# Banded attention: the meta keys' weights are transposed and multiplied last, the sample's loads get a step of their own, and the keys read their short block's product first

## The chip, the cores and the metric

The kernel runs on one core of one Trainium2 chip. The time is device microseconds (us) of one execution. Before the change the median of three runs is 2669.57 us (2669.01 to 2672.76). In the kernel's words PE is the engine of the matrix products, DVE the vector engine, ACT the scalar engine, POOL GpSimd, SP the queue that issues most transfers.

## What is computed

One step of a hybrid decoder trunk for 1024 prompt tokens behind 16 learned meta tokens, and for 8 sample sequences of 8 tokens, with the same weights: a half-step gated FFN, a token mixer (a gated delta rule branch A and a sliding-window attention branch B, merged by gates), and a second half-step FFN. The change touches the keys of branch A and all of branch B. Cut to these:

```python
# branch A, per head and chunk of c = 64 tokens
a_mat = where(strict, beta[..., :, None] * einsum('nzhid,nzhjd->nzhij', k, k) * decay, 0) + eye(c)
sol = triangular_solve(a_mat, rhs)          # the kernel inverts a_mat: its "lane solve"
# branch B, blocks of 128 queries: 16 meta keys, the block before, the own block, a sink
scores = concat([einsum('nbqkgd,nskd->nbkgqs', q, k_meta), einsum('nbqkgd,nbskd->nbkgqs', q, k_band)]) * scale
p = softmax(concat([where(mask, scores - slope * min(dist, 128), -inf), sink]))[..., :-1]
o = einsum('nbkgqs,nskd->nbqkgd', p[..., :16], v_meta) + einsum('nbkgqs,nbskd->nbqkgd', p[..., 16:], v_band)
y = sigmoid(gate_A) * o_A + sigmoid(gate_B) * o_B
```

There are 8 query heads of 128 on 2 key heads. The sample does the same with a cache of 128 past keys per sequence.

## The kernel before

A product in fp32 is made of three products of two-part operands (a high part and what is left of it, called the remainder here). Products that fill PE's time, the projections by weights (`gu`), are generators that yield after each matmul. `weave` takes several such generators, each with a stretch (a, b) and a count n, and interleaves their steps: `(g, 0.6, 1, 3)` puts three steps of g into the last 40% of the fill. So PE's program order is decided by these numbers and by the order of the yields. PE works in that order; the instructions of DVE, ACT and POOL are put in an order of their own by a scheduler that looks at the whole program, and each engine then works strictly in its order.

**Keys** (`keys`, `all_keys`, one head after another). For each head kT is transposed, its squared norms taken, and the Gram products of 9 token tiles weighted by the decay `dt`: `products(0)`, `products(4)` with four tiles each (PSUM tag `pk`), and `products(8)` for the short block of 80 tokens, whose Gram product already lies in a PSUM tile of tag `tr` (three buffers) with a transpose. DVE reads it there at L1058 (`b8`), and L1054 are the other eight tiles' reads. The next head's transposes (L1022) need a `tr` buffer.

**Banded attention** (`swa_block`, `swa_blocks`, `window`). There are 32 blocks: four passes p (two heads each) of 8 token blocks t. Block b does, in steps:

- scores: six matmuls (L1266 to L1268) into `sc`; DVE adds the distance term (L1269), takes the maximum (L1238) and its negative (L1239), ACT two exponentials (L1241), DVE a reciprocal (L1242), ACT two scalings (L1244); POOL splits the 16 meta weights into parts (`m3`, L1275 and L1276).
- meta: two transposes of `m3` (L1283) into a `pt` tile, which ACT copies out (L1285).
- own, then prev: two transposes (L1294) of the weights on the own and on the previous block into a `pt` tile each; ACT copies the high part out (L1296) and DVE the remainder (L1297, which reads `pt` and ACT's copy).
- po: the chain of seven matmuls (L1306) with the values into `po`; DVE multiplies by the gate (L1307).

Tag `pt` has two PSUM buffers, taken in turn: a third tile waits until all readers of the first are done. `swa_blocks` runs iteration i as: scores of block i, meta of block i-2, po of block i-3, own and prev of block i-2. In passes 0 to 2 these 5 steps are woven into 289 fill matmuls for 40 steps (7.2 each), in the last pass into 146 for 55 (the fill then takes 85% of the stretch).

Beside the blocks DVE does the lane solve (`lane_solve`, pairs of L1111 and L1113 of `ltmp` and `la`), until it is inverted and ACT copies it out in four parts (L1143). In passes 2 and 3 `swa_sample` is woven in, too: it loads queries (`q`, POOL's copies `qp`, L1332), scores of two halves (L1342), a softmax, then per half two transposes (L1357), the values' matmuls (L1366, L1369) into `po`, and a last transpose.

Of the kernel before, what the change touches and what calls it, by code (L numbers as in the profile page):

```python
# [13 lines left out]
ALU = mybir.AluOpType  # L14
# [4 lines left out]
P = 128  # L19
# [139 lines left out]
def steps_of(g, n):  # L159

    return itertools.islice(g, n)
# [573 lines left out]
class Mixer:  # L735
# [270 lines left out]
    def keys(self, h):  # L1006

        c, nc, pool = self.c, self.nc, self.kpool
        cv, dt = self.x[h]["cv"], self.x[h]["dt"]
        k8 = self.x[h]["k8"]  # L1010
        nc.sync.dma_start(self.kf_d[h][:, 0:1024], cv[:, 0:1024])
        nc.sync.dma_start(self.kf_d[h][:, 1024:NTOK], k8)
        kt = c.t(pool, [P, 9, P], tag="kt", bufs=2)
        sq = c.t(pool, [P, P], tag="sq", bufs=2)
        for t0 in (0, 4, 8):
            pt = self.ps([P, 4, P], "tr", 3)
            if t0 < 8:
                for t in range(t0, t0 + 4):
                    nc.tensor.transpose(pt[:, t - t0, :], cv[:, t * P:(t + 1) * P], self.k(C_IDENT))
                nc.scalar.copy(kt[:, t0:t0 + 4, :], pt)  # L1020
            else:
                nc.tensor.transpose(pt[:80, 0, :], k8, self.k(C_IDENT))  # L1022
                nc.tensor.matmul(pt[:80, 1, 0:80], k8, k8, start=True, stop=True)
                nc.gpsimd.memset(kt[64:P, 8, :], 0.0)
                nc.scalar.copy(kt[:80, 8, :], pt[:80, 0, :])
            if t0 < 8:
                yield
        ssq = c.t(pool, [P, 9], tag="ssq", bufs=2)
        for t in range(9):
# [12 lines left out]
        nc.gpsimd.tensor_tensor(out=nr, in0=nr, in1=c.half[:, 0:9], op=ALU.pow)  # L1042
        yield

        b = c.t(pool, [P, 8, P], tag="bm", bufs=2)

        def products(t0):
            if t0 < 8:
                pk = self.ps([P, 4, P], "pk", 2)
                for t in range(t0, t0 + 4):  # L1050
                    a = cv[:, t * P:(t + 1) * P]
                    nc.tensor.matmul(pk[:, t - t0, :], a, a, start=True, stop=True)
                for t in range(t0, t0 + 4):
                    nc.vector.scalar_tensor_tensor(out=b[:, t, :], in0=pk[:, t - t0, :], scalar=ns[:, t:t + 1],  # L1054
                                                   in1=dt[:, t, :], op0=ALU.mult, op1=ALU.mult)
            else:
                b8 = c.t(pool, [80, 80], tag="b8", bufs=2)
                nc.vector.scalar_tensor_tensor(out=b8, in0=pt[:80, 1, 0:80], scalar=ns[:80, 8:9], in1=dt[:80, 8, 0:80],  # L1058
                                               op0=ALU.mult, op1=ALU.mult)
                nc.sync.dma_start(self.b8_d[:, h, :], b8)  # L1060

        for t0 in (0, 4, 8):
            products(t0)
            if t0 == 8:
                for store in ((self.dt_d[h][:, 0:8, :], dt[:, 0:8, :]), (self.dt_d[h][0:80, 8, 0:80], dt[0:80, 8, 0:80])):
                    c.tc.keep_in_program_order(nc.sync.dma_start(*store))
                for half in range(2):
                    r = slice(half * 64, half * 64 + 64)
                    nc.sync.dma_start(self.la_d[h, :, half].rearrange("t r c -> r t c"), b[r, :, r])
                nc.sync.dma_start(self.bo_d[h], b[0:64, :, 64:128])  # L1070
            yield

    def all_keys(self):
        c = self.c
        with ExitStack() as ek:
# [3 lines left out]
            with ExitStack() as eg:  # L1079
# [6 lines left out]
                for h in range(H + 1):  # L1086
                    if 0 < h < H - 1:
                        self.sums(h + 1)
                    if 0 < h < H:
                        before.append((self.decays(h), 0.3, 0.4, 1))  # L1090
                    weave((fill[h], 0, 1, 73), *before)
                    if h < H:
                        self.keys_pack(h)
                    if h == 0:
                        self.sums(0)
                        self.sums(1)
                        drain(self.decays(0))
                    if h < H:
                        this = self.keys(h)
                        before = [(steps_of(this, 3), 0.03, 0.25, 3), (this, 0.6, 1, 3)]  # L1100


    def lane_solve(self, a, n, size, tmp):
# [142 lines left out]
    def swa_block(self, t, p, pool):  # L1246
# [31 lines left out]
        sg = c.t(pool, [P, 2, P], tag="sgb", bufs=2)  # L1278
        nc.sync.dma_start(sg, self.sg_d[hs, :, cols].rearrange("h p t -> p h t"))
        gs = slice(g * P, (g + 1) * P)  # L1280
        pt = self.ps([P, 4, P], "pt", 2)
        for i in range(2):
            nc.tensor.transpose(pt[:48, i, :], f32(m3[:, i]).rearrange("p a k -> p (a k)"), self.k(C_IDENT))  # L1283
        pm = self.pm[t % 2]
        nc.scalar.copy(pm[0:48], pt[:48, 0:2])  # L1285
        ops, late = [(self.vm[:, gs], pm)], []
        yield
        parts = [(own, t, "pto")]
        if t:
            parts.append((0, t - 1, "ptp"))  # L1290
# [10 lines left out]
            yield  # L1301
        if not t:
            yield
        po = self.ps([P, 4, P], "po")
        for k, (v, p_) in enumerate(ops + late):
            nc.tensor.matmul(po[:, 0:2], v, p_, start=k == 0, stop=k == len(ops + late) - 1)  # L1306
# [4 lines left out]
    def swa_blocks(self, pool):  # L1311
# [2 lines left out]
        part = lambda i, n: steps_of(bl[i], n) if 0 <= i < len(bl) else iter([None] * n)  # L1314
        for i in range(len(bl) + 3):
            yield from part(i, 1)
            yield from part(i - 2, 1)
            yield from part(i - 3, 1)
            yield from part(i - 2, 2)

    def swa_sample(self, g, pool, tmp):

# [12 lines left out]
        for half in range(2):  # L1335
            h4 = slice(4 * half, 4 * half + 4)
            kc = c.t(tmp, [P, 4, 152], tag="kc")
            nc.sync.dma_start(kc[:, :, 0:144], I["kcT"][:, g, h4])
            nc.gpsimd.tensor_copy(kc[:, :, 144:152], self.kn[:, g, 32 * half:32 * half + 32].rearrange("p (s t) -> p s t", t=8))
            ps = self.ps([P, 272], "sc", 2)  # L1340
            for i in range(4):
                nc.tensor.matmul(ps[32 * i:32 * i + 32, :152], qp[:, 4 * half + i, :], kc[:, i, :],  # L1342
# [37 lines left out]
    def window(self, pool, es):  # L1380
# [21 lines left out]
        for p in range(4):  # L1402
            side = []
            if p == 2:
                side = [(self.swa_sample(0, pool, c.pool(ss[0], "swat0")), 0, 1, 8)]
            if p == 3:
                el.close()
                self.hq = self.pcp = c.pool(es, "hq", side="right")
                self.pcs = 2
                fill = self.qv_steps(0, None)  # L1410
                side = [(self.swa_sample(1, pool, c.pool(ss[1], "swat1")), 0, 0.9, 8)]
            else:
                fill = solving(chained(*self.swa_q(2 * p + 2), *self.swa_q(2 * p + 3)), 0, 10)
            weave((fill, 0, 0.85 if p == 3 else 1, 146 if p == 3 else 289), (steps_of(blocks, 40 if p < 3 else 55), 0, 1, 40 if p < 3 else 55),
# [823 lines left out]
```

## Time and profile before

| | us |
|---|---|
| median of three runs | 2669.57 |
| the profiled execution's own time | 2665.62 |
| its span (first to last instruction) | 2663.8 |
| PE busy in it | 2593.7 |
| DVE busy | 1558.4 |
| ACT busy | 1130.7 |
| POOL busy | 1268.4 |

The rows that follow are of the profiled execution, with times in us from its start. The keys run about from 830 to 950, the blocks from 1010 to 1275. A row of a wait names the tile and line that waited, then the engine, tile and line that released it. A row of the timeline is: start, duration of one instruction, engine, line, operation, the tile written and the tile read, shape, and in brackets how long the engine was idle ahead of it and what ended that.

### The profile page before, as it was taken

How to read it: one execution, taken by the hardware profiler on the slowest of the kernel's cores; microseconds unless marked ns; L12 is line 12 of the kernel's file. 1: busy time of each engine (PE TensorE's matmuls, PEld its weight loads, DVE VectorE, ACT ScalarE, POOL GpSimd, SP SyncE). 2: the span in 40 equal slices, each digit the busy share in tenths (PEclk: the TensorE clock that was granted, in tenths of full speed). 3: DMA queues.
4: the chain of work that ended last, by engine and by line, in shares of the span. 5: the costliest groups of instructions: out<-in, count | busy, mean ns of one | idle time of the engine just before them, and what ended most of it. 6: DMA issues, size and time to landing. Idle time of an engine off the chain costs nothing.

```text
span 2663.8 us, 49377 instructions
## 1 busy us (share of the span) xinstructions
PE 2593.7 (97%) x18993; PEld 2475.1 (93%) x18993; DVE 1558.4 (59%) x2315; ACT 1130.7 (42%) x2728; POOL 1268.4 (48%) x1205
## 2 busy tenths in 40 slices
PE   7999999999999999999999999999899999999998
PEld 7999999999988999888889999997699999999998
DVE  7657565545677726995454444444466656554566
ACT  6333343432145634457444444454443434334221
POOL 6656555445524533433343333435565555554471
PEclk9999999999999999999999999999999999999999
DMA  4344343667544744335333333335443434338764
GB/s 164 121 152 152 127 167 117 242 227 253 190 151 151 230 148 130 106 122 176 98 106 88 89 95 99 100 93 160 138 132 140 167 127 149 127 137 319 244 225 145
DMA packets 231570, 406.48 MB, mean 153 GB/s; under 512 B 61814, under 2 KB 123414, under 8 KB 231046
## 3 DMA queue, kind: packets, MB, share of 16 engines
q1 hardware_dynamic: 211030, 324.75, 38.0%
q10 hardware_dynamic: 20304, 78.56, 7.5%
q8 instruction: 150, 2.46, 0.4%
q14 instruction: 86, 0.70, 0.1%
HBM read 264.36 MB, written 140.53 MB: 152 GB/s over the span
## 4 chain that ended last, share of the span: by engine, by line
PE 47%; DVE 1%; ACT 1%; POOL 1%; issue 1%; DMA 0%; POOLq 0%; DVEq 0%; SPq 0%; ACTq 0%
PE y L532 9%; PE B L352 7%; PE C L352 5%; PE A L352 4%; PE gu L132 4%; PE gu L128 4%; PE gu L130 4%; PE dn L128 1%; PE dn L132 1%; PE dn L130 1%; PE ch L1651 1%; PE tr L1527 1%; PE ch L1656 0%; PE oq L1646 0%; PE on L1673 0%
## 5 line engine op out<-in xcount | busy, mean ns | idle before, releaser
L132 PE MATMUL gu<-xh,wl 128*128 128x512 f32 (+3 forms) x1456 | 495.7, 340 | 0.0
L128 PE MATMUL gu<-xh,wh 128*128 128x512 f32 (+3 forms) x1456 | 491.9, 338 | 0.0
L130 PE MATMUL gu<-xl,wh 128*128 128x512 f32 (+3 forms) x1456 | 490.6, 337 | 0.0
L318 POOL TENSOR_TENSOR wl<-T,wh 128x512 fp32r<-128x512 f32 x246 | 330.5, 1350 | 314.1 <-ACT wh L317 244.4
L532 PE MATMUL y<-hb,wh 128*128 128x256 f32 (+2 forms) x2528 | 430.6, 290 | 2.1 <-ACT acc L572 1.0
L318 POOL TENSOR_TENSOR wl<-raw,wh 128x512 fp32r<-128x512 f32 x200 | 282.9, 1423 | 249.0 <-ACT wh L317 191.1
L532 PEld LDWEIGHTS y<-hb,wh 128*128 128x128 f32 x2528 | 366.1, 189 | 3.2 <-ACT acc L572 1.2
L317 ACT CAST wh<-T 128x512 fp32r<-128x512 f32 x246 | 152.2, 620 | 362.5 <-PE B L352 110.4
L132 PEld LDWEIGHTS gu<-xh,wl 128*128 128x128 f32 x1456 | 276.9, 190 | 16.4 <-issue 0.4
L130 PEld LDWEIGHTS gu<-xl,wh 128*128 128x128 f32 x1456 | 276.9, 190 | 16.3 <-issue 0.4
L128 PEld LDWEIGHTS gu<-xh,wh 128*128 128x128 f32 x1456 | 276.7, 190 | 16.4 <-issue 0.9
L532 PE MATMUL y<-hb,wl 128*128 128x256 f32 (+2 forms) x1264 | 271.8, 289 | 0.0
L317 ACT CAST wh<-raw 128x512 fp32r<-128x512 f32 x200 | 122.4, 621 | 276.8 <-PE C L352 81.9
L806 POOL TENSOR_TENSOR wl<-raw,wh 128x1024 fp32r<-128x1024 f32 x58 | 141.0, 2431 | 180.6 <-ACT wh L805 161.5
L543 DVE TENSOR_TENSOR acc<-acc,y 128x552 f32<-128x552 f32 (+4 forms) x216 | 144.9, 679 | 139.0 <-PE y L532 138.7
L532 PEld LDWEIGHTS y<-hb,wl 128*128 128x128 f32 x1264 | 207.1, 188 | 0.0
L292 DVE TENSOR_TENSOR T<-raw,raw 128x512 f32<-128x512 f32 x124 | 117.0, 948 | 107.1 <-POOL wl L318 107.1
L1606 POOL TENSOR_TENSOR f<-f,mhalf 128x1 f32<-128x1 f32 (+1 forms) x72 | 54.8, 762 | 125.5 <-DVE f L1604 119.2
L303 DVE TENSOR_TENSOR T<-raw,T 128x512 f32<-128x512 f32 x62 | 65.5, 1059 | 61.8 <-POOL wl L318 61.4
L292 DVE TENSOR_TENSOR T<-raw,T 128x512 f32<-128x512 f32 x62 | 63.3, 1028 | 31.9 <-POOL wl L318 31.5
L966 DVE SCALAR_TENSOR_TENSOR cv<-pc,cw,cv 128x1131 f32<-128x1131 f32 x48 | 66.8, 1393 | 21.4 <-POOL cv L963 20.8
L1111 DVE TENSOR_TENSOR ltmp<-la 72x14 f32<-72x14 f32 (+37 forms) x76 | 72.1, 948 | 12.3 <-DMA la<-b_d 11.4
(612 smaller groups left out, 7298.1 us busy)
## 6 DMA issues: line engine op xcount, KB each, us to landing
hb<-hid SPq DMA_DIRECT2D x71, 552.0 KB
hb<-hid SPq DMA_DIRECT2D x71, 544.0 KB
hid<-hs ACTq DMA_DIRECT2D x69, 552.0 KB
hid<-hs ACTq DMA_DIRECT2D x69, 544.0 KB
raw<-in_w_in_dram SPq DMA_DIRECT2D x58, 512.0 KB
raw<-in_ffn_w_gate_dram SPq DMA_DIRECT2D x100, 256.0 KB
raw<-in_ffn_w_up_dram SPq DMA_DIRECT2D x94, 256.0 KB
raw<-in_ffn_w_down_dram SPq DMA_DIRECT2D x88, 256.0 KB
```

The costliest lines, as they stand in the source:

```text
L128: nc.tensor.matmul(ps, wh, xh, start=first and i == 0, stop=False)
L130: nc.tensor.matmul(ps, wh, xl, start=False, stop=False)
L132: nc.tensor.matmul(ps, wl, xh, start=False, stop=last and i == n - 1)
L292: pin(self.nc.vector.tensor_tensor(out=b[name], in0=b[x], in1=b[y], op=ALU.subtract))
L317: self.nc.scalar.copy(hi, s)
L318: self.nc.gpsimd.tensor_tensor(out=lo, in0=s, in1=f32(hi), op=ALU.subtract)
L352: self.nc.tensor.matmul(self.view(ps, (i,)), w[a][:, k * P:(k + 1) * P], self.X[p][i][b][:, k, :], start=first and k + a + b == 0, stop=k ...
L532: self.nc.tensor.matmul(self.view(ps[d], (i,)), w[x][:, d * P:(d + 1) * P], hb[:, y, lo:hi], start=j + x + y == 0, stop=j == len(items) - ...
L543: dve = lambda out, x, y: nc.vector.tensor_tensor(out=out, in0=x, in1=y, op=ALU.add)
L806: low.tensor_tensor(out=lo, in0=raw, in1=f32(hi), op=ALU.subtract)
L966: nc.vector.scalar_tensor_tensor(out=cv, in0=pc[:, w:w + PADW], scalar=self.cw[:, j, w:w + 1], in1=cv, op0=ALU.mult, op1=ALU.add)
L1111: pin(nc.vector.tensor_tensor(out=t, in0=a[:n, 0:j, j:j + 1].to_broadcast([n, j, w]), in1=a[:n, j:j + 1, j + 1:size].to_broadcast([n, j, w ...
```

## The change

In `swa_block` the meta step is moved behind own and prev, and its product moves to the end of the chain of po. In `swa_blocks` an iteration becomes: scores i, po i-3, own i-2, prev i-2, meta i-2. In `swa_sample` a yield is added ahead of the first half's score matmuls, so the sample has one step more and all its later steps stand elsewhere in the fill. In `keys` the short block's read is emitted ahead of `products(0)`, the stores go with `products(4)`, and there are two steps for three, at 0.55 to 0.95.

```diff
         def products(t0):
-            if t0 < 8:
-                pk = self.ps([P, 4, P], "pk", 2)
...
-            else:
-                b8 = c.t(pool, [80, 80], tag="b8", bufs=2)
...
-        for t0 in (0, 4, 8):
-            products(t0)
...
+        b8 = c.t(pool, [80, 80], tag="b8", bufs=2)
+        nc.vector.scalar_tensor_tensor(out=b8, in0=pt[:80, 1, 0:80], scalar=ns[:80, 8:9], in1=dt[:80, 8, 0:80],
+                                       op0=ALU.mult, op1=ALU.mult)
+        nc.sync.dma_start(self.b8_d[:, h, :], b8)
+        products(0)
+        yield
+        products(4)
...
-                        before = [(steps_of(this, 3), 0.03, 0.25, 3), (this, 0.6, 1, 3)]
+                        before = [(steps_of(this, 3), 0.03, 0.25, 3), (this, 0.55, 0.95, 2)]
...
-        pt = self.ps([P, 4, P], "pt", 2)
-        for i in range(2):
-            nc.tensor.transpose(pt[:48, i, :], f32(m3[:, i]).rearrange("p a k -> p (a k)"), self.k(C_IDENT))
-        pm = self.pm[t % 2]
-        nc.scalar.copy(pm[0:48], pt[:48, 0:2])
-        ops, late = [(self.vm[:, gs], pm)], []
-        yield
+        ops, late = [], []
         parts = [(own, t, "pto")]
...
+        pt = self.ps([P, 4, P], "pt", 2)
+        for i in range(2):
+            nc.tensor.transpose(pt[:48, i, :], f32(m3[:, i]).rearrange("p a k -> p (a k)"), self.k(C_IDENT))
+        pm = self.pm[t % 2]
+        nc.scalar.copy(pm[0:48], pt[:48, 0:2])
+        late.append((self.vm[:, gs], pm))
+        yield
         po = self.ps([P, 4, P], "po")
...
             yield from part(i, 1)
-            yield from part(i - 2, 1)
             yield from part(i - 3, 1)
-            yield from part(i - 2, 2)
+            yield from part(i - 2, 3)
...
+            if not half:
+                yield
             ps = self.ps([P, 272], "sc", 2)
...
-                side = [(self.swa_sample(0, pool, c.pool(ss[0], "swat0")), 0, 1, 8)]
+                side = [(self.swa_sample(0, pool, c.pool(ss[0], "swat0")), 0, 1, 9)]
...
-                side = [(self.swa_sample(1, pool, c.pool(ss[1], "swat1")), 0, 0.9, 8)]
+                side = [(self.swa_sample(1, pool, c.pool(ss[1], "swat1")), 0, 0.9, 9)]
```

Line numbers shift with it: L1287 of the changed kernel is L1294 of before, L1299 is L1283, L1265 is L1266, L1142 is L1143, L1240 is L1241, L1243 is L1244, L1289 is L1296, L1301 is L1285, L1053 is L1054.

PE around block 12 (its weights are s_13027, its meta parts m_1949_13048), in the second pass, before; the lines left out are fill matmuls and the rest of each chain:

```order
L1283 MATMUL pt_13287<-ident_62,m_1949_13048 48x128 x2
...
L1306 MATMUL po_13300<-ptm_1643_11198,vm_11196 128x256
...
L1306 MATMUL po_13300<-ptpl_13225,vth_11193 128x256
...
L1294 MATMUL pt_13323<-ident_62,s_13027 128x128 x2
...
L1294 MATMUL pt_13337<-ident_62,s_13027 128x128 x2
...
L1266 MATMUL sc_13361<-kxh_11190,qbh_13355 128x272
...
L1283 MATMUL pt_13395<-ident_62,m_1969_13156 48x128 x2
```

The same place in the changed kernel:

```order
L1306 MATMUL po_13285<-ptpl_13212,vth_11193 128x256
L1306 MATMUL po_13285<-ptm_1643_11198,vm_11196 128x256
...
L1287 MATMUL pt_13306<-ident_62,s_13027 128x128 x2
...
L1287 MATMUL pt_13326<-ident_62,s_13027 128x128 x2
...
L1299 MATMUL pt_13340<-ident_62,m_1949_13048 48x128 x2
...
L1265 MATMUL sc_13361<-kxh_11190,qbh_13355 128x272
```

The meta transposes of a block moved from the step after the scores of two blocks on to the fourth step after them; own and prev stand one step earlier than they did, and the third `pt` tile in a row is now taken by meta two steps behind own.

ACT near the last copies of the lane solve (`ltmp`), where block 21's own and prev tiles are copied out (ptoh, ptph); s_2209 holds the weights of a later block; before:

```order
L1285 CAST ptm1_1643_11198<-pt_2216_14346 48x256
L1143 COPY ltmp_1633_11185<-la_1632_11184 128x1024
L1241 ACTIVATE s_2209_14312,dnb_2213_14325<-s_2209_14312,nmb_2212_14324 128x273 x2
L1244 ACTIVATE s_2209_14312<-s_2209_14312,dnb_2213_14325 128x272 x2
L1296 CAST ptoh_2222_14384<-pt_2221_14381 128x256
L1143 COPY ltmp_1633_11185<-la_1632_11184 128x1024
L1296 CAST ptph_2225_14398<-pt_2224_14395 128x256
```

and in the changed kernel:

```order
L1301 CAST ptm0_1642_11197<-pt_2205_14295 48x256
L1142 COPY ltmp_1633_11185<-la_1632_11184 128x1024
L1255 CAST qbh_2257_14521<-qb_2256_14519 128x256
L1227 ACTIVATE qe_2216_14354<-gu_2199_14267 128x256
L1240 ACTIVATE s_2209_14312,dnb_2213_14325<-s_2209_14312,nmb_2212_14324 128x273 x2
L1142 COPY ltmp_1633_11185<-la_1632_11184 128x1024
L1289 CAST ptoh_2220_14370<-pt_2219_14367 128x256
L1243 ACTIVATE s_2209_14312<-s_2209_14312,dnb_2213_14325 128x272 x2
L1289 CAST ptph_2224_14387<-pt_2223_14384 128x256
```

The last copy of the lane solve moved from behind own's copy `ptoh` to ahead of it.

DVE in the keys of head 0, where b_1472 and b_1469 are the short block's read, as a piece of the difference:

```order
 L1037 TENSOR_TENSOR sd_9799<-s__1445_9699,dec_9686 128x9
-L1054 SCALAR_TENSOR_TENSOR bm_9853<-pk_9854,ns__1446_9700,dt_9721 128x128 x2
+L1053 SCALAR_TENSOR_TENSOR bm_9849<-pk_9853,ns__1446_9700,dt_9721 128x128 x2
 L1038 TENSOR_TENSOR kt_9755<-kt_9755,sd_9799 128x1152
 L994 TENSOR_TENSOR dt_9723<-dt_9723,cst_9420 128x1024
 L996 TENSOR_TENSOR dt_9723<-dt_9723,cst_9420 80x80
-L1054 SCALAR_TENSOR_TENSOR bm_9853<-pk_9854,ns__1446_9700,dt_9721 128x128 x2
-L1054 SCALAR_TENSOR_TENSOR bm_9853<-pk_9872,ns__1446_9700,dt_9721 128x128 x4
-L1058 SCALAR_TENSOR_TENSOR b_1472_9891<-tr_9780,ns__1446_9700,dt_9721 80x80
+L1053 SCALAR_TENSOR_TENSOR bm_9849<-pk_9853,ns__1446_9700,dt_9721 128x128 x2
+L1053 SCALAR_TENSOR_TENSOR bm_9849<-pk_9879,ns__1446_9700,dt_9721 128x128 x3
+L1058 SCALAR_TENSOR_TENSOR b_1469_9850<-tr_9780,ns__1446_9700,dt_9721 80x80
```

Though it is written first, the short block's read stands only one tile's read earlier in DVE's order than before.

## Rows read from the trace of the kernel before

**Rows 1.** The page: busy us of each engine, share, instructions.

```profile
PE 2593.7 (97%) x18993; PEld 2475.1 (93%) x18993; DVE 1558.4 (59%) x2315; ACT 1130.7 (42%) x2728; POOL 1268.4 (48%) x1205
```

**Rows 2.** Waits of PE, 730 to 1285: us in total, times, longest.

```profile
PE pt L1283 <- POOL m L1276: 2.9, 2, 2.1
PE tr L1022 <- DVE b L1058: 2.7, 1, 2.7
PE sc L1342 <- POOL qp L1332: 2.7, 1, 2.7
PE po L1366 <- DVE sgb L1307: 2.0, 2, 1.4
...
PE pt L1357 <- ACT s L1244: 1.4, 1, 1.4
...
PE pt L1283 <- POOL m L1275: 0.7, 1, 0.7
PE pt L1283 <- DVE nms L1239: 0.7, 1, 0.7
PE pt L1283 <- DVE ptol L1297: 0.7, 1, 0.7
```

**Rows 3.** Windows: length, busy us of PE, PEld, DVE, ACT, POOL; clock; DMA.

```profile
1030.00:1092.00 62.00, 59.11 (x394) 55.09 (x393) 58.82 (x98) 29.17 (x90) 25.24 (x29) 0.97 0.37 115
1092.00:1154.00 62.00, 60.52 (x405) 55.25 (x405) 61.78 (x94) 32.09 (x98) 29.39 (x28) 1.00 0.37 116
```

**Rows 4.** Windows behind long waits of PE, same columns (clock is third from last).

```profile
847.48:850.88 3.40, 3.40 (x12) 2.83 (x11) 3.33 (x4) 1.74 (x8) 1.42 (x2) 0.50 0.95 241
1069.34:1072.74 3.40, 3.40 (x16) 3.40 (x15) 3.40 (x6) 0.36 (x1) 0.32 (x1) 0.50 0.40 118
1178.57:1181.97 3.40, 3.40 (x16) 3.32 (x15) 2.36 (x4) 1.37 (x4) 0.85 (x2) 0.50 0.45 127
1221.20:1229.00 7.80, 5.14 (x35) 4.17 (x36) 5.26 (x10) 2.86 (x11) 4.77 (x14) 1.00 0.83 242
```

**Rows 5.** Timeline of DVE in the keys of head 0.

```profile
844.69 1.63 DVE L1054 SCALAR_TENSOR_TENSOR bm<-pk,ns__1446_9700,dt 128x128 f32<-128x128 f32 x6
846.25 0.28 DVE L1058 SCALAR_TENSOR_TENSOR b<-tr,ns__1446_9700,dt 80x80 f32<-80x80 f32 x1
```

**Rows 6.** Timeline of PE and DVE: block 12's prev transposes, its own remainder.

```profile
1134.34 0.38 PE L1294 MATMUL pt<-ident,s 128*128 128x128 f32 x2
...
1137.44 0.42 DVE L1297 TENSOR_TENSOR ptol<-pt,ptoh 128x256 fp32r<-128x256 f32 x1
```

**Rows 7.** Timeline of PE, DVE and ACT at the first sample's softmax.

```profile
1172.54 0.29 PE L1268 MATMUL sc<-kxh,qbl 128*128 128x272 f32 x1
...
1174.04 0.92 DVE L1113 TENSOR_TENSOR la<-la,ltmp 128x686 f32<-128x686 f32 x1
...
1167.68 0.73 ACT L1244 ACTIVATE s<-s,dns 128x152 f32<-128x152 f32 x2 [2.52 <-DVE dns L1242]
```

**Rows 8.** Timeline of PE, ACT and POOL at the lane solve's last copy.

```profile
1216.22 0.38 PE L1294 MATMUL pt<-ident,s 128*128 128x128 f32 x2
...
1217.34 2.03 ACT L1143 COPY ltmp<-la 128x1024 f32<-128x1024 f32 x1 [0.36 <-DMA lrt_d<-ltmp]
1219.27 0.37 ACT L1296 CAST ptph<-pt 128x256 fp32r<-128x256 f32 x1
...
1223.05 0.76 POOL L1332 COPY qp<-q 128x64 f32<-128x64 f32 x4
```

**Rows 9.** Timeline of PE and ACT in the last pass: blocks 25 and 28.

```profile
1226.43 0.28 PE L1266 MATMUL sc<-kxh,qbh 128*128 128x272 f32 x1
1241.46 0.28 PE L1266 MATMUL sc<-kxh,qbh 128*128 128x272 f32 x1
...
1231.45 0.51 ACT L1241 ACTIVATE s<-s,nmb 128x273 f32<-128x273 f32 x1
1244.80 0.51 ACT L1241 ACTIVATE s<-s,nmb 128x273 f32<-128x273 f32 x1
```

More of the change, by code (lines that the diff above doesn't have):

```diff
@@ L1047, in products @@
         def products(t0):
-            if t0 < 8:
-                pk = self.ps([P, 4, P], "pk", 2)
[L1050 to L1055, printed above, removed]
-            else:
-                b8 = c.t(pool, [80, 80], tag="b8", bufs=2)
-                nc.vector.scalar_tensor_tensor(out=b8, in0=pt[:80, 1, 0:80], scalar=ns[:80, 8:9], in1=dt[:80, 8, 0:80],
-                                               op0=ALU.mult, op1=ALU.mult)
-                nc.sync.dma_start(self.b8_d[:, h, :], b8)
@@ L1062, in keys @@
-        for t0 in (0, 4, 8):
-            products(t0)
[L1064 to L1070, printed above, removed]
-            yield
+            pk = self.ps([P, 4, P], "pk", 2)
@@ new lines, in products @@
+            for t in range(t0, t0 + 4):
+                a = cv[:, t * P:(t + 1) * P]
+                nc.tensor.matmul(pk[:, t - t0, :], a, a, start=True, stop=True)
+            for t in range(t0, t0 + 4):
+                nc.vector.scalar_tensor_tensor(out=b[:, t, :], in0=pk[:, t - t0, :], scalar=ns[:, t:t + 1],
+                                               in1=dt[:, t, :], op0=ALU.mult, op1=ALU.mult)
+        b8 = c.t(pool, [80, 80], tag="b8", bufs=2)
+        nc.vector.scalar_tensor_tensor(out=b8, in0=pt[:80, 1, 0:80], scalar=ns[:80, 8:9], in1=dt[:80, 8, 0:80],
+                                       op0=ALU.mult, op1=ALU.mult)
@@ new lines, in keys @@
+        nc.sync.dma_start(self.b8_d[:, h, :], b8)
+        products(0)
+        yield
+        products(4)
+        for store in ((self.dt_d[h][:, 0:8, :], dt[:, 0:8, :]), (self.dt_d[h][0:80, 8, 0:80], dt[0:80, 8, 0:80])):
+            c.tc.keep_in_program_order(nc.sync.dma_start(*store))
+        for half in range(2):
+            r = slice(half * 64, half * 64 + 64)
+            nc.sync.dma_start(self.la_d[h, :, half].rearrange("t r c -> r t c"), b[r, :, r])
+        nc.sync.dma_start(self.bo_d[h], b[0:64, :, 64:128])
@@ L1280, in swa_block @@
         gs = slice(g * P, (g + 1) * P)
-        pt = self.ps([P, 4, P], "pt", 2)
-        for i in range(2):
-            nc.tensor.transpose(pt[:48, i, :], f32(m3[:, i]).rearrange("p a k -> p (a k)"), self.k(C_IDENT))
-        pm = self.pm[t % 2]
-        nc.scalar.copy(pm[0:48], pt[:48, 0:2])
-        ops, late = [(self.vm[:, gs], pm)], []
-        yield
+        ops, late = [], []
         parts = [(own, t, "pto")]
@@ L1339, in swa_sample @@
             nc.gpsimd.tensor_copy(kc[:, :, 144:152], self.kn[:, g, 32 * half:32 * half + 32].rearrange("p (s t) -> p s t", t=8))
+            if not half:
+                yield
             ps = self.ps([P, 272], "sc", 2)
```

## Prediction

> **What bounds the kernel now.** The page comes first: PE is busy 2593.7 of 2663.8 us, DVE 1558.4, ACT 1130.7 [rows 1]. Over the whole, PE is the bound, and a change that neither adds nor removes matmuls, as this one, can only move what PE waits. So the second view is PE's waits from the keys to the last block [rows 2]. Those the change can reach are: one of 2.7 us in the keys (next head's transposes behind the short block's read), meta transposes behind POOL (2.9 in two) and once each behind `m` of L1275, `nms` and `ptol` (0.7 each), the second sample's scores behind `qp` (2.7), the first sample's product behind `sgb` (2.0 in two), and its transposes behind the softmax (1.4). Together 13.8 us, half a per cent of the time, are at stake. The third view, the windows, shows that the stages differ: from 1092 to 1154 DVE is busy 61.78 of 62.00 us, and 58.82 in the 62 us ahead [rows 3]. There DVE's order decides, and PE's waits are symptoms. The fourth shows the clock: behind three of the waits the granted clock stands for 3.4 us at 0.50, the 1.2 GHz level, so each such stretch costs half of it, 1.7 us of work; behind the 2.7 us wait for `qp` it stays at 1.00, the 2.4 GHz level [rows 4].
>
> **The change part by part.** The sum is made against the profiled execution's own time of 2665.62 us, which lies 3.95 under the median of the runs, 2669.57.
>
> *Keys.* The same instructions remain. The short block's read stands in DVE's order behind the decay's last instruction as before, and one of the six tile reads ahead of it has gone behind. Six take 1.63 us [rows 5], so it comes 1.63 / 6 = 0.27 earlier: the wait of 2.7 shrinks to about 2.4, and I leave the slow clock behind it where it is. −0.3 us; the bounds are 0 and −4.4 (wait and slow stretch both gone: 2.7 + 1.7).
>
> *Meta last, in passes 0 to 2.* The two transposes, the ACT copy and the product of each block are only moved. What is new is which buffer they need. Of the two `pt` tiles in turn, meta of block b now takes the one of own of block b, two steps earlier, and so waits for DVE's remainder of own (L1297). Before, own's tile was taken again by the next block's meta, behind scores, po and the rest. Where DVE has slack this is nothing: a step is 7.2 fill matmuls, and 40 steps fill a pass. Where DVE is saturated it is late. Block 12 shows by how much: meta now stands where prev's transposes stood, at 1134.34, while own's remainder ended at 1137.44 + 0.42 = 1137.86 [rows 6]. That is 3.5 us later than PE would get there. Such a wait comes once and not per block, since in a stretch that DVE bounds, PE once late stays late by the same amount. Before, PE already stood 0.8 us for DVE's chain there (the second wait behind `m` of L1276, 2.9 − 2.1 [rows 2]), which the new wait contains: +3.5 − 0.8 = +2.7 us. The other meta waits (2.1 + 0.7 + 0.7) are part of PE's following DVE, and stay in another place. The bounds are −4.3 (2.1 + 0.8 + 0.7 + 0.7: DVE's order comes to suit the new place, all of them go) and +5.2 (3.5 in full, and one slow stretch of 1.7 behind it).
>
> *First sample.* With a ninth step its transposes stand right behind the scores that ran at 1172.54 [rows 7]. PE gets there at 1172.8 − 1.4 (the old wait is ahead no more) + 2.7 (the wait above) = 1174.1. In the changed DVE order the sample's reciprocal stands behind the solver's update of 686 elements, which ended at 1174.04 + 0.92 = 1174.96; the two scalings on ACT took 0.73, so the weights are ready at 1175.7 [rows 7]. New wait 1.6 for old 1.4: +0.2. The sample's product leaves the place right behind a block's po and comes 26 fills later (counted in PE's order before and behind, 691 to 717 from the first scores on), so that the waits for `sgb`, 2.0 [rows 2], go. I take −1.8; the bounds are −5.1 (1.4 + 2.0 + 1.7 for the slow stretch at 1178, which has then no wait ahead of it) and +2 (one more such stretch).
>
> *Block 21 and the lane solve's copies.* Meta of block 21 now stands where transposes ran at 1216.22. It needs own's copy on ACT, which now stands behind the solver's last copy: that began at 1217.34 and took 2.03, then a copy of 0.37 [rows 8] and a remainder of 0.42 [rows 6], ready at 1220.2. PE, late by the net of the terms above (−0.3 + 2.7 − 1.8 = +0.6), comes at 1216.8: +3.4 us. The scores of the second sample go from fill 870 to 886 of the same count, 16 fills on. The copies of `qp` end at 1223.05 + 0.76 = 1223.8 [rows 8], and 16 fills of a pass with 3 per step are five steps, a whole block, of which each takes 5.0 us there (below). So the wait of 2.7 goes. Net +0.7; bounds −2.7 (the copy hidden) and +3.4.
>
> *Last pass.* Scores of block 25 ran at 1226.43, of block 28 at 1241.46 [rows 9]: 15.03 / 3 = 5.0 us a block, so the four steps from the scores of block b+2 to the meta of b take 4.0. In ACT's changed order own's copy of b stands in five blocks (22, 23, 25, 26, 27) behind the exponentials of b+2. Those of block 28 ended at 1244.80 + 0.51 = 1245.31; with copy and remainder (0.37 + 0.42) meta could go at 1246.1, 4.6 after the scores: a wait of 0.6. Those of block 25 ended at 1231.96, which makes 6.3 and a wait of 2.3. I take the lower row, because a wait at one block lets ACT catch up for the next: 5 × 0.6 = 3.0, less the old wait for `nms` of 0.7 [rows 2]: +2.3. Bounds: −0.7 and 5 × 2.3 − 0.7 = +10.8.
>
> Sum: −0.3 + 2.7 − 1.8 + 0.7 + 2.3 = +3.6 us, 0.13%: 2665.6 becomes 2669.2, and the median 2673.2.
>
> Transfers are not changed: the short block's store and the others are issued in the same number, the first a little earlier, and no queue of theirs releases PE in [rows 2].
>
> **The rivals.** *The waits go and no new ones come (faster).* The schedule of DVE and ACT was made for the new order, and the rows above are read at the old one's times. If own's remainder is placed two solver instructions earlier (they take about 1 us each, as the 0.92 of [rows 7]), three quarters of block 12's lateness is gone, and there the sign turns. Then the meta waits (2.1 + 0.8 + 0.7 + 0.7 + 0.7 = 5.0), `qp` (2.7) and `sgb` (2.0) go: −9.7, 2659.9 on the median. For it speaks that each of them is a wait with one releaser which the change moves away from; against it the saturated window [rows 3].
>
> *The two buffers bind in every block of the last pass (slower).* If each of the five blocks waits as block 25's rows say, that term is +10.8 in place of +2.3, and the sum is +12.1: 2681.7. It decides from about 1 us a block on (5 × 1.0 − 0.7 and the other +1.3 are over 5.3). For it: PE's step is only 0.8 us there, less than a DVE or ACT hold-up of one long instruction (2.03 in [rows 8]). Against it: a late PE also gives ACT time. The Trainium skill, page "Perfetto Trace Analysis", section "Optimization Strategy", says that a gap that repeats on the engine that should be saturated can mean too little PSUM for the next tile, by its buffer count. By it this change, which brings the reuse of a two-buffer tile nearer to its readers, would show the same small gap in block after block; no row of before shows such a row of gaps, and whether the changed kernel does is what separates this rival.
>
> *It does nothing* (all new places hidden, old waits moved elsewhere): within 1 us of 2669.6. For it: most terms are differences of an old and a new wait of like size.
>
> **How the numbers follow.** My forecast +3.6 (its own range −1 to +6) gets 0.42, nothing 0.10, the faster rival 0.22, the slower one 0.26. A measurement of this kernel can tell about 0.2%, 5.3 us, from no change. The forecast and nothing lie within that (0.52 less a little for the forecast's upper edge, which about makes up for the rivals' weak forms), so: faster 0.22, same 0.50, slower 0.28. The range reaches to the middle of both rivals, 2660 to 2681, which leaves out half of each, 0.24; I keep it there, for weak forms of either fall inside.
>
> **What would show it.** Right: a wait of PE for `ptol` at the meta transposes (L1299 of the changed kernel) of 2 to 4 us near 1120 to 1140, and one near 1220 behind ACT's copy out of the lane solve; several of 0.3 to 1 us at the meta transposes after 1230; no wait for `qp` or `sgb`; a wait of about 2.4 still at the keys' transposes behind `b`. Wrong: no wait at the meta transposes at all (faster rival), over 1.5 us at most of them after 1225 (slower), more or fewer than three or four stretches at clock 0.50, each worth 1.7 us, or a keys' wait that is gone because DVE reaches the short block ahead of `dt`'s last part.

## The result, and the profile after

The changed kernel takes 2678.41 us (median of 7 runs, 2673.3 to 2680.93) against 2669.57 for the kernel before in the same session: a ratio of 1.0033, 95% interval 1.0024 to 1.0042. It is 8.8 us slower. That is inside the stated range (2660 to 2681), but beyond the 0.2% up to which the prediction spoke of "same", its largest chance, and above the forecast's own range (+3.6, with −1 to +6).

The page of the changed kernel, busy us of each engine, answers to [rows 1]:

```profile
span 2674.0 us, 49361 instructions
PE 2596.8 (97%) x18993; PEld 2474.6 (93%) x18993; DVE 1559.8 (58%) x2315; ACT 1132.6 (42%) x2728; POOL 1269.3 (47%) x1205
```

The work is the same, the span is 10.2 us longer (2674.0 for 2663.8). To see where, I take the start of the same fill matmul (the n-th projection matmul, 4752 in each) in both traces, at the borders of the stages:

```text
place                                   before     after   after - before
end of FFN1                             760.93    761.14   +0.21
keys done, ahead of the blocks         1010.06   1009.64   -0.42
ahead of the sample's second scores    1162.32   1163.91   +1.59
first sample's product done            1189.99   1191.16   +1.17
blocks 18 to 20 done                   1214.39   1218.46   +4.07
second sample's first scores           1227.18   1231.69   +4.51
last block done                        1291.89   1299.42   +7.53
end of the next stage                  1662.97   1670.17   +7.21
```

So 8.0 us arise between the blocks' start and their end (from −0.42 to +7.53). The other 2.7 of this pair of executions come after 1820 us, in code that the change doesn't touch. The profiled execution of before lies 3.95 under its median, so that the medians' 8.8 is the better number for the whole and the table for the places.

PE's waits in the blocks' stretch (1005 to 1285; us in total, times, longest), which answer to [rows 2]:

```profile
PE pt L1299 <- DVE ptol L1290: 8.4, 9, 2.0
PE pt L1299 <- ACT pts L1362: 3.0, 2, 1.7
PE sc L1343 <- POOL m L1274: 2.1, 1, 2.1
PE pt L1299 <- DVE nmb L1238: 2.1, 2, 1.3
PE pt L1299 <- DVE ptpl L1290: 1.1, 1, 1.1
PE pt L1299 <- DVE dnb L1241: 1.0, 1, 1.0
PE pt L1287 <- DVE sg L1377: 0.4, 1, 0.4
```

The waits for `qp`, `sgb` and the sample's softmax are gone, as are those for `m`. In their place the meta transposes (L1299) wait 15 times, 15.6 us in all: 8.4 + 3.0 + 2.1 + 1.1 + 1.0. In nine of them the releaser named is the remainder of own (`ptol`), the last reader of the tile that was filled two steps earlier. It is the true one in three more: the rows name `dnb` or `nmb`, which a meta transpose doesn't read, but own's remainder ends 0.14 to 0.15 ahead of these transposes, too (at 1083.34, 1091.37 and 1265.31, for starts at 1083.49, 1091.51 and 1265.46). The other three, 4.1 us, are for prev's tile (below). So all fifteen are waits for a tile to come free, twelve for own's (11.5 us), three for prev's.

The stretches at half clock from the keys to the last block, which answer to [rows 4] (the clock is the third number from the right):

```profile
846.97:850.38 3.41, 3.41 (x12) 2.82 (x11) 3.34 (x4) 1.77 (x8) 1.43 (x2) 0.50 0.91 241
1167.82:1171.23 3.41, 3.41 (x13) 2.98 (x12) 2.96 (x8) 1.12 (x4) 0.54 (x1) 0.50 0.67 216
1222.43:1225.85 3.42, 3.38 (x13) 3.17 (x14) 0.73 (x2) 2.47 (x7) 1.69 (x4) 0.50 1.02 293
```

Three, as before. The one at 1069 has gone with its wait, the one at 1178 stands at 1168, and one has come behind block 21's wait.

The keys, DVE and PE, which answer to [rows 5]:

```profile
844.45 1.37 DVE L1053 SCALAR_TENSOR_TENSOR bm<-pk,ns__1446_9700,dt 128x128 f32<-128x128 f32 x5
845.75 0.28 DVE L1058 SCALAR_TENSOR_TENSOR b<-tr,ns__1446_9700,dt 80x80 f32<-80x80 f32 x1
...
846.18 0.28 PE L1022 MATMUL tr<-ident,k 128*80 128x128 f32 x1 [2.43 <-POOL kt L1024]
```

Five tile reads stand ahead of the short block's in place of six, and the wait is 2.43 for 2.73: the 0.3 forecast. The bracket names a memset on POOL, but PE starts 0.15 after the short block's read ends (845.75 + 0.28 = 846.03), as it did before (846.25 + 0.28, then 846.68): the releaser is still `b`.

The saturated stretch: meta of block 10 and what it waits for, which answer to [rows 6]:

```profile
1119.07 0.38 PE L1299 MATMUL pt<-ident,m 128*48 128x128 f32 x2 [1.50 <-DVE ptol L1290]
...
1117.42 1.17 DVE L1110 TENSOR_TENSOR ltmp<-la 128x990 f32<-128x990 f32 x1
1118.50 0.42 DVE L1290 TENSOR_TENSOR ptol<-pt,ptoh 128x256 fp32r<-128x256 f32 x1
```

Here the forecast's mechanism is seen in one place: the remainder stands behind a solver product, ends at 1118.92, and PE goes on 0.15 later. Before, it stood behind the same product, which came 1.5 us later:

```profile
1118.91 1.19 DVE L1111 TENSOR_TENSOR ltmp<-la 128x990 f32<-128x990 f32 x1
1120.02 0.42 DVE L1297 TENSOR_TENSOR ptol<-pt,ptoh 128x256 fp32r<-128x256 f32 x1
```

And block 12, whose rows the forecast was made from:

```profile
1136.73 0.38 PE L1299 MATMUL pt<-ident,m 128*48 128x128 f32 x2 [1.17 <-DVE ptol L1290]
...
1136.18 0.40 DVE L1290 TENSOR_TENSOR ptol<-pt,ptoh 128x256 fp32r<-128x256 f32 x1
```

The first sample, whose second half's scores now follow block 18's scores by four fill matmuls ([rows 7] is of its softmax):

```profile
1167.12 0.47 PE L1343 MATMUL sc<-kc,qp 128*32 128x152 f32 x8 [2.12 <-POOL m L1274]
...
1163.50 3.17 DVE L1110 TENSOR_TENSOR ltmp<-la 128x752 f32<-128x752 f32 x1
1166.59 0.77 DVE L1268 SCALAR_TENSOR_TENSOR s<-scst,sc 128x272 f32<-128x272 f32 x2
...
1163.49 2.38 POOL L806 TENSOR_TENSOR wl<-raw,wh 128x1024 fp32r<-128x1024 f32 x1 [4.61 <-ACT wh L805]
```

The bracket again names the wrong one (`m` isn't read by this matmul). What it needs is a score tile: both were taken by block 18, and DVE reads the first of them only at 1166.59, behind a solver product of 3.17 us. The products of 782 and 720 elements around it took 0.96 and 0.90; this one began 0.01 after a weight split on POOL. Behind the wait comes a stretch at half clock. Such a meeting isn't new; the trace of before has one near there, at which PE did not need a score tile (DVE, then POOL):

```profile
1163.37 2.58 DVE L1111 TENSOR_TENSOR ltmp<-la 128x782 f32<-128x782 f32 x1
...
1162.72 2.41 POOL L806 TENSOR_TENSOR wl<-raw,wh 128x1024 fp32r<-128x1024 f32 x1 [7.34 <-ACT wh L805]
```

Block 19, with a tile of the sample between its prev and its meta (PE, then ACT, then DVE):

```profile
1199.56 0.38 PE L1287 MATMUL pt<-ident,s 128*128 128x128 f32 x2
1200.21 0.27 PE L1358 MATMUL pt<-ident,s 128*128 128x128 f32 x1
...
1202.90 0.38 PE L1299 MATMUL pt<-ident,m 128*48 128x128 f32 x2 [1.72 <-ACT pts L1362]
...
1199.24 2.02 ACT L1142 COPY ltmp<-la 128x1024 f32<-128x1024 f32 x1
1201.17 0.93 ACT L1243 ACTIVATE s<-s,dnb 128x272 f32<-128x272 f32 x2
1202.00 0.35 ACT L1289 CAST ptph<-pt 128x256 fp32r<-128x256 f32 x1
...
1202.38 0.42 DVE L1290 TENSOR_TENSOR ptpl<-pt,ptph 128x256 fp32r<-128x256 f32 x1 [2.59 <-ACT ptph L1289]
```

The sample's transposes (L1358) took own's tile in the turn of two, so meta has to take prev's, which was written 0.7 us ahead of the sample's and not two steps earlier. Prev's copy waits on ACT behind a copy of the lane solve of 2.02 and two scalings, the remainder ends at 1202.80, and PE goes on at 1202.90.

Block 21, which answers to [rows 8]:

```profile
1222.47 0.59 PE L1299 MATMUL pt<-ident,m 128*48 128x128 f32 x2 [2.01 <-DVE ptol L1290]
...
1219.65 1.94 ACT L1142 COPY ltmp<-la 128x1024 f32<-128x1024 f32 x1 [1.71 <-DMA lrt_d<-ltmp]
1221.50 0.36 ACT L1289 CAST ptoh<-pt 128x256 fp32r<-128x256 f32 x1
...
1221.89 0.42 DVE L1290 TENSOR_TENSOR ptol<-pt,ptoh 128x256 fp32r<-128x256 f32 x1 [3.10 <-ACT ptoh L1289]
```

This is the chain of the forecast, step for step: solver's last copy, own's copy, remainder, meta.

The last pass, which answers to [rows 9]:

```profile
1246.64 0.38 PE L1299 MATMUL pt<-ident,m 128*48 128x128 f32 x2 [1.27 <-ACT pts L1362]
1265.46 0.38 PE L1299 MATMUL pt<-ident,m 128*48 128x128 f32 x2 [1.31 <-DVE nmb L1238]
...
1263.66 1.32 DVE L970 SCALAR_TENSOR_TENSOR qv<-th,qv 128x1131 f32<-128x1131 f32 x1
1264.90 0.41 DVE L1290 TENSOR_TENSOR ptol<-pt,ptoh 128x256 fp32r<-128x256 f32 x1
```

Two waits of 1.3 and two of 0.2 and 0.4, not one in every block. The first stands again behind a tile of the sample, the second behind own's remainder (the bracket names `nmb`), which itself stands behind a long DVE instruction of the next stage.

### The profile page after: what moved, and what is told of

The parts are those of the page before. It is cut to its first block, busy times and chain, and to the rows that moved or that the text cites. A ratio compares the mean times of both kernels' runs of the same rounds, so it can differ in the third digit from the quotient of the medians.

```text
span 2674.0 us, 49361 instructions
## 1 busy us (share of the span) xinstructions
PE 2596.8 (97%) x18993; PEld 2474.6 (93%) x18993; DVE 1559.8 (58%) x2315; ACT 1132.6 (42%) x2728; POOL 1269.3 (47%) x1205
## 4 chain that ended last, share of the span: by engine, by line
PE 47%; POOL 1%; issue 1%; DMA 1%; ACT 1%; DVE 1%; SPq 0%; DVEq 0%; POOLq 0%; ACTq 0%
PE y L532 8%; PE B L352 7%; PE C L352 5%; PE A L352 4%; PE gu L132 4%; PE gu L128 4%; PE gu L130 4%; PE dn L128 1%; PE dn L132 1%; PE dn L130 1%; PE tr L1528 1%; PE ch L1652 1%; PE on L1674 1%; PE oq L1647 0%; PE ch L1657 0%
## 5 line engine op out<-in xcount | busy, mean ns | idle before, releaser
L805 ACT CAST wh<-raw 128x1024 fp32r<-128x1024 f32 x60 | 62.9, 1049 | 36.4 <-PE gu L130 36.4
```

## The experiments

Theory A, which I held on seeing this: meta's new place asks for a PSUM tile soon after its last readers, and that lateness is the cost; the sample's tiles in the same turn shorten it further. Theory B: the sample's new step is what costs. All runs are against the kernel before in the same session; a ratio of 0.001 is 2.7 us. The microseconds given behind a ratio are worked out from it and differ from the difference of the medians by up to 2.

**The parts alone.** First the attention blocks' order alone, on the kernel before:

```diff
-        ops, late = [(self.vm[:, gs], pm)], []
-        yield
+        ops, late = [], []
...
+        late.append((self.vm[:, gs], pm))
+        yield
         po = self.ps([P, 4, P], "po")
...
-            yield from part(i - 2, 1)
             yield from part(i - 3, 1)
-            yield from part(i - 2, 2)
+            yield from part(i - 2, 3)
```

> The kernel before with the new order in the attention blocks alone (meta turned and multiplied last; sample and keys as before). Theory A, the tile: meta's transposes now wait for DVE's remainder of own in one of the two pt buffers, and that is most of the change's cost; it expects +5 to +8 us on before, with eight or more waits of PE for ptol at the meta transposes, in the trace some 8 us in total. Theory B, the sample: its new step costs most (a wait of 2.1 for the score tile and 3.0 for its copies pts), so this kernel is at most +3 us.

Measured 2675.23, ratio 1.0021 (1.0012 to 1.0029), +5.6 us. PE's waits there, 820 to 1330:

```profile
PE pt L1300 <- DVE ptol L1291: 8.7, 9, 1.9
...
PE sc L1342 <- POOL qp L1332: 2.2, 1, 2.2
PE pt L1357 <- ACT s L1244: 1.9, 1, 1.9
PE pt L1357 <- DVE ptol L1291: 1.7, 1, 1.7
```

The nine waits for `ptol` are there without the sample's edit, and the sample's two old waits remain. Theory A holds for this part, at the lower end of what it expected.

The sample's step alone:

```diff
+            if not half:
+                yield
...
-                side = [(self.swa_sample(0, pool, c.pool(ss[0], "swat0")), 0, 1, 8)]
+                side = [(self.swa_sample(0, pool, c.pool(ss[0], "swat0")), 0, 1, 9)]
```

> The kernel before with the sample's extra step alone. Theory A: -3 to +1 us on before: the wait for qp (2.7) goes, and what comes at other places of the sample is no more than that. Theory B: +4 to +7 us, with waits of PE at the sample's scores and at transposes behind its copies, and a stretch at half clock behind the longest.

Measured 2667.39, ratio 0.9987 (0.9979 to 0.9996), 3.5 us faster. Theory B falls as it was stated: by itself the step helps. What it costs beside the new order is a question of its own (below).

The keys alone:

```diff
-        for t0 in (0, 4, 8):
-            products(t0)
...
+        nc.sync.dma_start(self.b8_d[:, h, :], b8)
+        products(0)
+        yield
+        products(4)
...
-                        before = [(steps_of(this, 3), 0.03, 0.25, 3), (this, 0.6, 1, 3)]
+                        before = [(steps_of(this, 3), 0.03, 0.25, 3), (this, 0.55, 0.95, 2)]
```

> The kernel before with the edit of the keys alone. Both theories: within 1 us of before, the wait at the second head's transposes about 2.4 in place of 2.7. A third, that the keys cost (another slow stretch, a later store): +2 us or more.

Measured 2670.76, ratio 1.0003 (0.9994 to 1.0011): nothing. And the whole change with the attention order of before put back:

```diff
-        ops, late = [], []
+        ops, late = [(self.vm[:, gs], pm)], []
+        yield
...
             yield from part(i, 1)
+            yield from part(i - 2, 1)
             yield from part(i - 3, 1)
-            yield from part(i - 2, 3)
+            yield from part(i - 2, 2)
```

> The changed kernel with the attention blocks' order of before: the edits of keys and sample alone. By the single runs -3 us against before (-3.4 for the sample, 0 for the keys), if nothing between these two adds to it.

Measured 2668.16, ratio 0.9995 (0.9986 to 1.0003), −1.3 us with an interval that takes in both −3 and nothing. What matters is the sum: alone, the parts make +5.6 − 3.5 + 0.8 = +2.9 us; together +8.8. About 6 us come from the edits meeting; by the intervals of the four runs that could be 1 to 11, so it needed a run of its own (the sample's tiles, below). Said by this run: the order costs 5.6 alone, and 1.0033 − 0.9995 = 0.0038, 10.1 us, where the sample's step and the keys are there, too.

**The tile.** To take meta off the pair, its transposes were written into the free half of prev's tile:

```diff
-        pt = self.ps([P, 4, P], "pt", 2)
         for i in range(2):
-            nc.tensor.transpose(pt[:48, i, :], f32(m3[:, i]).rearrange("p a k -> p (a k)"), self.k(C_IDENT))
+            nc.tensor.transpose(pt[:48, 2 + i, :], f32(m3[:, i]).rearrange("p a k -> p (a k)"), self.k(C_IDENT))
```

> The changed kernel, but meta's transposes are written into the free half of prev's pt tile, so that meta takes no buffer of its own and doesn't wait for own's remainder; all else as changed. Theory A: the waits of meta for ptol, ptpl and pts (12.5 us in the trace) go or shrink to what the softmax leaves, and the time falls by 5 to 9 us below the changed kernel, to that of before or a little under. If it is DVE's and ACT's lateness itself that PE follows, whatever the tile, or the sample's step (theory B), it falls by less than 3 us.

Measured 2703.73, ratio 1.0133 (1.0119 to 1.0147), +35.5 us. My expectation was wrong. PE's waits, 820 to 1330:

```profile
PE pt L1298 <- DVE ptpl L1290: 32.5, 24, 3.4
PE pt L1298 <- DVE ptol L1290: 4.4, 3, 1.6
```

Columns that nobody reads don't help: meta's write still waits for the readers of the other half of that tile, and these are now one step behind and not two. As an experiment on distance it is clear: two steps cost 8.4 us in nine waits, one step 32.5 in 24.

Then meta in the one buffer of `po`, whose last reader (the gate's product) belongs to a step three earlier, so that own and prev have the pair for themselves:

```diff
-        pt = self.ps([P, 4, P], "pt", 2)
+        pt = self.ps([P, 4, P], "po")
         for i in range(2):
             nc.tensor.transpose(pt[:48, i, :], f32(m3[:, i]).rearrange("p a k -> p (a k)"), self.k(C_IDENT))
```

> The changed kernel, but meta's transposes take the one buffer of po (read by the gate's product three steps earlier) and not a pt tile; own and prev then have the two pt tiles for themselves, and a tile is taken again a whole block later. Theory A, the tile: meta's waits for ptol, ptpl and pts (12.5 us in the changed kernel's trace) mostly go, some come back at po behind ACT's copy of meta or at meta behind the gate's product; 4 to 9 us below the changed kernel. If PE only follows DVE's and ACT's lateness, whatever the tile: within 2 us of the changed kernel, with waits of the same size at po for own's remainder.

Measured 2673.96, ratio 1.0014 (1.0006 to 1.0023): +3.7 us on before, some 5 below the changed kernel. PE's waits, 1005 to 1285:

```profile
PE po L1306 <- ACT ptm L1301: 6.0, 7, 2.1
PE po L1367 <- ACT ptm L1301: 2.5, 1, 2.5
```

No meta transpose waits for a remainder, but the chain of po now waits for ACT to have emptied meta's tile: less, not nothing.

**The sample's tiles.** The sample's transposes in score tiles, all else as changed:

```diff
-            pt = self.ps([P, 4, P], "pt", 2)
+            pt = self.ps([P, 272], "sc", 2)[:, 0:256].rearrange("p (a b) -> p a b", b=P)
...
-            px = self.ps([P, 4, P], "pt", 2)[:, 0]
+            px = self.ps([P, 272], "sc", 2)[:, 0:P]
```

> The changed kernel, but the sample's transposes take score tiles (tag sc) and not pt tiles. The two edits made alone sum to about +2 us and together to +8.8. If that is since the sample's tile comes between prev and meta in the turn of two, so that meta takes prev's tile one step behind it (waits behind ptpl and pts, 4.1 us in the trace): 3 to 6 us below the changed kernel. If the sum comes from the order that DVE and ACT got, and not from the tile: within 2 us of the changed kernel.

Measured 2674.6, ratio 1.0013 (1.0005 to 1.0022): +3.5 on before, 5.3 below the changed kernel, near the 6 us that the edits' meeting had cost. Not all of that gain need be the meeting's: in the old order the same move stands at 0.9981 (below) against 0.9987 for the sample's step alone, 1.6 us, though these two are not told apart. PE's waits from 1185 to 1238, the changed kernel first, then this one:

```profile
PE pt L1299 <- DVE ptol L1290: 2.0, 1, 2.0
PE pt L1299 <- ACT pts L1362: 1.7, 1, 1.7
PE pt L1299 <- DVE ptpl L1290: 1.1, 1, 1.1
```

```profile
PE pt L1299 <- DVE ptol L1290: 1.6, 2, 0.8
```

The waits behind prev are gone with the sample's tile from the turn, block 21's is 0.8 for 2.0, and the half-clock stretch at 1222 is not there (in this execution another stands at 1294, behind the blocks). The sample's own wait of 2.1 at its second scores is the same as before the move. Both moves at once:

> Both of the last two: meta in po's bank, the sample in score tiles, so that own and prev alone use pt. By theory A it is the fastest of the kernels with the new order, 6 to 11 us below the changed kernel, and at or under before. If po's single buffer, which now carries three kinds of tiles, binds: no better than with meta alone moved.

Measured 2672.41, ratio 1.0011 (1.0003 to 1.002): 5.9 below the changed kernel, not told apart from either alone, and not under before. The po chain's waits for `ptm` are the same (5.7 in seven, and 2.4 at the sample's product). So its single buffer still costs what it cost with meta alone moved.

**The copies on ACT.** The lane solve's four last copies on DVE:

```diff
-                nc.scalar.copy(at, a[:, :, 16 * q:16 * q + 16].rearrange("p r c -> p c r"))
+                nc.vector.tensor_copy(at, a[:, :, 16 * q:16 * q + 16].rearrange("p r c -> p c r"))
```

> The changed kernel with the four last copies of the lane solve on DVE and not on ACT. In its trace meta of blocks 19 and 21 waits 1.7 and 2.0 us, with the copies of own or prev behind such a copy of 2.0 us on ACT, and the second wait has a stretch at half clock behind it. Theory A with the copies: these waits shrink below 0.8 together, and the time falls by 3 to 5 us. If the hold-up only moves to DVE, where the remainder waits behind the copies: within 2 us of the changed kernel.

Measured 2675.34, ratio 1.0021 (1.0012 to 1.0029), 3.2 us below the changed kernel, with intervals that overlap. From 1185 to 1238:

```profile
PE pt L1299 <- DVE ptol L1290: 1.4, 2, 1.1
PE pt L1299 <- DVE ptpl L1290: 1.1, 1, 1.1
PE pt L1358 <- DVE ptol L1290: 0.3, 1, 0.3
```

Block 19's wait is gone, block 21's is 1.1 and not below the 0.8 expected, so part of it seems to have moved to DVE. With the sample in score tiles as well:

> The changed kernel with the sample in score tiles and the lane solve's copies on DVE. If both hold-ups are separate, 1 to 3 us below the changed kernel with the sample in score tiles alone (2674.6), as only block 21's wait of 0.8 and what the clock makes of it is left there; what then stays above before, 1 to 3 us, is meta's wait for own's remainder in the saturated stretch and in the last pass.

Measured 2671.83, ratio 1.0003 (0.9994 to 1.0011): no longer told from before.

**The order of before, with what helped.** The sample's step and its score tiles, with attention and keys as before; then the copies on DVE, too:

> The kernel before with the sample's extra step and the sample's transposes in score tiles: attention and keys as before. The sample's step alone gave -3.4 us and its trace keeps waits of 1.5, 1.0 and 0.8 at pt tiles that the sample takes. If these were due to the shared pair, they go, and this is -4 to -7 us on before, the fastest so far; if the score tiles make as many waits, -3 as before.

> The kernel before with the sample's step, the sample in score tiles and the lane solve's copies on DVE. With the attention order of before, meta asks for its tile late, so the copies on ACT cost nothing there: within 1.5 us of the same kernel with the copies on ACT. If the copies hold up ACT whatever the order, 2 to 4 us below it.

Measured 2666.35, ratio 0.9981 (0.9973 to 0.999), and 2664.86, ratio 0.998 (0.9969 to 0.999): both faster than before, by about 5 us, and not told apart from each other (nor, by their intervals, from the sample's step alone). The three waits named for the sample's tiles (1.5, 1.0 and 0.8) are gone in both traces; two at score tiles, of 0.8 and 0.65, have come. In this order the copies on ACT cost nothing that can be seen.

Each of these two has a partner with the changed order (and the changed keys), which gives the price of the order twice more: with the sample in score tiles 1.0013 − 0.9981 = 0.0032, 8.5 us; with the copies on DVE as well 1.0003 − 0.998 = 0.0023, 6.1 us. So the order costs 5.6 alone, 10.1 beside the sample's step, 8.5 when the sample's tiles are away from the pair and 6.1 when the copies are away from ACT, too. That is the row which theory A expects. But each of the three differences is sure to some 3 us only, so that no step of the row is shown by its time alone.

## Why the prediction was right or wrong

Point by point, the forecast's terms against the table of places:

| term | forecast | in the traces |
|---|---|---|
| keys | −0.3 | −0.4 up to the blocks (the wait −0.3; run alone, nothing) |
| blocks ahead of the sample's second scores | +2.7 | +2.0 |
| first sample | −1.8 | −0.4 |
| blocks 18 to 20 | no term | +2.9 |
| block 21 and `qp` | +0.7 | +0.4 |
| last pass | +2.3 | +3.0 |
| sum | +3.6 | +7.5; medians +8.8 |

- *What bounds and what meta waits for* was right. The wait for own's remainder in a pair of buffers is the new order's cost: 8.4 us of waits, +5.6 us with that part alone. In the saturated stretch it doesn't add up block by block: eight waits of 0.4 to 1.5 there, 7.6 us, which take the place of before's 4.3 and of the half-clock stretch at 1069, make +2.0. The wait at block 12 is 1.17 and not the 3.5 that I had priced (nor the 2 to 4 named as a sign). PE came there 1.2 us later than I had it, at 1136.73 − 1.17 = 1135.56 for 1134.34, and own's remainder ended 1.3 earlier, at 1136.18 + 0.40 = 1136.58 for 1137.86. The remainder's place in DVE's order is not the reason: at blocks 10 and 12 it stands behind the same solver product as before, and the whole lane solve runs 1.3 to 1.5 us earlier there. Why it does, no run tells.
- *Block 21* was right as a chain, mis-sized in its parts: 2.0 for 3.4, and a half-clock stretch behind it, 1.7, which I had put in no term. `qp` went, as forecast.
- *The step that failed* is "First sample". It says of the ninth step only what becomes of the sample's own waits. I had followed meta's tile through own and prev, and not asked who else takes that tag, nor what the sample's scores take theirs from. The sample's tiles are in the same turn of two: wherever one now stands between prev and meta, meta is one step behind its tile's readers and not two (blocks 18 and 19: 1.1 and 1.7; in the last pass 1.3). And its second scores stand right behind a block's in the pair of score tiles (2.1, with a half-clock stretch in place of the one at 1178). In the table the forecast fell 3.9 us short: these two places came out 4.3 above it (−0.4 for −1.8, and +2.9 where no term stood), all others together 0.4 below. The rows show the waits, and in the run with the sample's tiles taken away the three behind prev's tile (4.1 us) are gone. How much of the 5.3 us which that run gained is the meeting of the two edits is open, as the same move may have given 1.6 in the old order. A count was wrong, too: the sample's first product moved by 19 fills (698 to 717 in the traces) and not by 26; that its waits for `sgb` go held all the same.
- *The last pass* came near in size by luck, as the waits are others: not five blocks behind exponentials, but one behind the sample's tile, one behind a 1.3 us DVE instruction of the next stage, and two small ones.
- *The slower rival* foresaw the side and not the mechanism: not five blocks of 2.3 in the last pass. (Its 0.8 us for a step there doesn't fit the 5.0 for the five steps of a block, which makes 1.0.) The Trainium skill, "Perfetto Trace Analysis", section "Optimization Strategy", says that the same gap repeating on the engine that should be saturated can mean too little PSUM for the next tile; the twelve waits for own's tile and three for prev's agree, spread over all passes, and it deserved more weight than I gave that rival. *The faster rival*'s gains came (`qp` and `sgb`, 4.7 us, and the old meta waits, 5.0), and 15.6 us at one line came in their place.
- *The range* held by its width. It reached to the middle of the slower rival, whose mechanism did not come; +8.8 is outside the −1 to +6 of the forecast itself.

What stays open: whether a third `pt` tile would make the new order free. No run has one; meta in po's bank moved the wait to po and came to +3.7. Nor can I say how much of each difference comes from the order of DVE and ACT, which changes with every edit here. That a half-clock stretch costs its 1.7 us at each of these places was taken from the rows and not tested by itself.

## What to carry to other kernels

Before a step is moved that takes a tile from a turn of buffers, write down the whole turn, with everybody who takes that tag, and count for each tile the steps between its last reader and its next writer; a side stream that puts one tile into a turn of two halves that distance at its place. Price two edits that share such a turn together: here −3.5 and +5.6 (and +0.8 for the keys, which is nothing by its interval) made +8.8. And where several edits come as one change, run each alone before keeping it: the sample's step was worth keeping, and with the sample in score tiles it beats both kernels (0.9981).

## What the runs showed of the hardware

- A write to columns of a PSUM tile that nobody reads waited for the readers of the tile's other columns (24 waits, 32.5 us). Whether that is the chip's or the schedule's doing the runs don't tell.
- The same DVE product, of 752 elements, took 3.17 us where it began with a POOL weight split of 2.38 us, and 0.93 in the trace of before, where nothing ran on POOL beside it. It ended 0.80 us after the split did; before's product of 782 elements that began 0.65 into a split took 2.58, and ended 0.82 after it. A wait of 2.1 on PE hung on that meeting; it comes again in the traces of the three other kernels that keep the changed order and meta in `pt`, and change the sample's tiles or the copies (2.1 in each).
- Stretches at half clock of the same code differ between executions: near 62 us, where all these kernels run the same code, it lasted 3.41 us in the profiled execution of before and 6.83 in that of the attention order alone. Half of the difference is 1.7 us, and with another such stretch near 27 us that execution was 2.7 us later at 760 us. A difference of 2 us between two single executions tells nothing here.
